# One tile of the way down, from ahead of the third product to behind the fourth, in 18 blocks of a gated MLP

## The chip, the cores and the metric

The kernel runs on one core of one Trainium2 chip. The metric is the device time of one execution in microseconds. The engines of a core run side by side, each through its own list of instructions in order, and wait for one another by semaphores: TensorE (PE in the rows; its weight loads, PEld, overlap with the matmuls), VectorE (DVE), ScalarE (ACT), GpSimd (POOL) and SyncE (SP), which issues the DMAs.

## The reference

One layer of a trunk on x of 1024 tokens by 1024 features in float32: two kinds of attention that share their projections, then a gated MLP. Each part stands behind a norm that is modulated by a conditioning vector. The change lies in the MLP:

```
h = modulate(rms_norm(x), shift_ffn, scale_ffn)
gate, val = split(causal_depthwise_conv(h @ w_up, conv_w, conv_b), 2)   # 2 x 2816 features, width 3 along tokens
x = x + gate_ffn * ((silu(gate) * val) @ w_down)
return rms_norm(x) * final_g
```

## The kernel before

Float32 is kept up by splitting each operand into a high and a low part that TensorE reads as float32r: a product of two operands is three matmuls (high by high, low by high, high by low). `h` lies in SBUF with features on the partitions and tokens along the row, in two halves of 512 tokens, 128 features a piece.

The MLP runs over 22 blocks. Block `fb` makes 128 gate features and 128 value features for all tokens (the way up), applies the convolution, SiLU and the gate, and leaves activations of 128 features by 1024 tokens. These are multiplied with the 128 rows of `w_down` that belong to them (the way down) during the next block. The way down of a block is 16 tiles, each of 128 tokens by 512 output features: three matmuls into a PSUM bank `dnf` (`down_mm`, `mm3g`, L137), and an add of that bank onto `x2` by VectorE (L1231). There are four `dnf` banks, taken in turn.

From block 2 on, the way up of a block (`act_fast`) is a 2 by 2 product (gate and value by two token halves, over two halves of the 1024 input features) done in the manner of Winograd and Strassen: seven products in place of eight. Sums of input halves (`T1`, `T2`, `T4`) are made once, sums of weight quarters for each block by `weight_sums`. A product is 12 matmuls of 128 x 512 (`product`, L1095) into one of four PSUM banks `up`, here called X, Y, W and Z:

- first, into X; ScalarE copies X out (L1121). Second, into Y; VectorE adds it to that copy (L1131), which gives the gate's first token half.
- third, adds into X; ScalarE copies X (L1137). Fourth, adds into X again; ScalarE copies X (L1146).
- fifth, into W; VectorE subtracts it (L1152): the value's first half. Sixth, into Z; VectorE subtracts it (L1162): the value's second half. Seventh, adds into Z; VectorE subtracts it (L1173): the gate's second half.

Behind each of the four results comes its convolution: one pass on ScalarE (L1100) and two on VectorE (L1104). Behind the gate's halves comes SiLU (L1139, L1180). `gated` multiplies gate and value (L1037, VectorE), splits off the high part (L1038, ScalarE) and the low part (L1039, VectorE); for the second token half this is left to the next block, between its first and second product (`rest`).

Between the products stand tiles of the way down of the block before. How many behind which product is a table: entry 0 behind the second product, 1 behind the third, 2 behind the fourth, 3 behind the fifth, 4 behind the sixth; four more stand behind the seventh and none behind the first. Block 2 has its own row of the table (`NTWO`), block 21 too (`NLAST`); the 18 blocks from 3 to 20 use `NDOWN`. The order of the tiles among themselves is fixed: the first four are token tiles 0 to 3 with the first half of the output features, the fifth to eighth the same tokens with the second half, and so on. All of this is kept in the order in which it is written (`ko`).

```
    n = NLAST if last else NTWO if fb == 2 else NDOWN
    ...
    def tiles(n, c=iter(()), dn=dn):
        for _ in range(n):
            nx(dn)
            nx(c)
    ...
    if fb > 2:
        nx(c)
    tiles(n[0], c)
    product(X, w[4], T2, False)
    ko(sc.copy(cg[:, hi], X))
    run(c, 9)
```

`c` is the convolution of the gate's first half: a step of it is taken behind each tile, and what is left of it behind the third product.

Of the kernel before, what the change touches and what calls it, by code (L numbers as in the profile page):

```python
# [26 lines left out]
NP = 8  # L27
FF = 2816
NF = FF // P
NDOWN = 2, 3, 2, 2, 3  # L30
NLAST = 2, 2, 0, 0, 0
NTWO = 0, 4, 2, 3, 3
TL = sum(NLAST)
# [22 lines left out]
def build(nc, tc, t, ctx):  # L56
# [3 lines left out]
    def mk(pool, shape, dt, tag):  # L60
        cnt[0] += 1
        return pool.tile(shape, dt, name=f"{tag}_{cnt[0]}", tag=tag, bufs=BUFS.get(tag, 1))
# [1043 lines left out]
    def act_fast(fb, w, dn, nw, nw1, ld, ld1, act, after, last):  # L1106
# [3 lines left out]
        lo, hi = slice(0, HALF), slice(HALF, S)  # L1110
        n = NLAST if last else NTWO if fb == 2 else NDOWN
        cg, cv = (mk(p2, [P, S], F32, "y") for _ in range(2))
# [379 lines left out]
```

## Time and profile before

| | us |
|---|---|
| median of 3 runs | 1384.16 (1381.42 to 1384.59) |
| the profiled execution | 1383.4 |
| its span, first to last instruction | 1381.6 |
| mean granted TensorE clock | 0.983 of full speed |

The way up and down of the blocks 3 to 20 takes from about 780 us to 1335 us of the span. In rows of the timeline and of the chain the first number is the start in us from the span's start, the second the duration. A matmul's row is longer than its share, as matmuls are pipelined: the distance from one start to the next counts.

### The profile page before, as it was taken

To read this page: it belongs to the slowest core of one execution; us is meant where nothing else is said; L and a number is where in the kernel's file an instruction comes from. 1 tells how busy PE (TensorE), PEld (TensorE's weight loads), DVE (VectorE), ACT (ScalarE), POOL (GpSimd) and SP (SyncE) were. 2 spreads that over 40 slices of the span, in tenths; PEclk is the share of its full clock that TensorE was granted. 3 is DMA by queue.
4 is the path that set the end of the run, shared out by engine and by line. 5 is a ranking of instruction groups with operands and counts; after the bars stand their busy time and mean duration, and the time that the engine had idled before them with its cause. 6 is when DMAs were issued, how large, how long until landed. Compare 5 with 4: busy or idle time off the path is not lost.

```text
span 1381.6 us, 19584 instructions
## 1 busy us (share of the span) xinstructions
PE 1292.6 (94%) x6596; PEld 1072.4 (78%) x6596; DVE 1097.3 (79%) x1896; ACT 651.9 (47%) x1332; POOL 841.2 (61%) x746
## 2 busy tenths in 40 slices
PE   5999999999999979999888999999999999999996
PEld 3897988798788967877666888887888888878874
DVE  7769888788777747857897888888878888888777
ACT  6666656566555544534423333433333334333335
POOL 2157677776543436644686776676667766766754
PEclk9999999999999999999999999999999999999998
DMA  8725444535573586681101111111111111121113
GB/s 332 237 59 137 139 130 124 157 104 145 130 182 105 165 206 209 198 274 61 53 15 46 46 46 59 50 59 63 46 47 46 46 52 56 55 62 53 46 38 123
DMA packets 73169, 145.09 MB, mean 105 GB/s; under 512 B 11114, under 2 KB 21482, under 8 KB 73068
## 3 DMA queue, kind: packets, MB, share of 16 engines
q1 hardware_dynamic: 73068, 143.83, 35.0%
q8 instruction: 53, 0.87, 0.3%
q14 instruction: 48, 0.39, 0.1%
HBM read 103.41 MB, written 18.88 MB: 89 GB/s over the span
## 4 chain that ended last, share of the span: by engine, by line
PE 38%; DVE 29%; ACT 7%; POOL 4%; DMA 4%; issue 3%; SPq 1%; POOLq 0%; ACTq 0%; DVEq 0%
PE up L1095 14%; PE mm L137 9%; PE dnf L137 8%; DVE y L1104 6%; DVE x L1231 4%; PE T L137 4%; DVE y L1037 4%; ACT y L1100 3%; PE S L137 2%; DVE al L1039 2%; ACT ah L1038 1%; POOL pb L780 1%; POOL wl L122 1%; DMA rawm<-ada 1%; DVE y L1282 1%
## 5 line engine op out<-in xcount | busy, mean ns | idle before, releaser
L1231 DVE TENSOR_TENSOR x<-dnf,x 128x512 f32<-128x512 f32 x340 | 226.0, 682 | 10.0 <-PE dnf L137 10.0
L1061 POOL TENSOR_TENSOR wl<-raw,wh 128x1024 fp32r<-128x1024 f32 (+1 forms) x62 | 160.0, 2582 | 76.7 <-ACT wh L1059 75.3
L1095 PE MATMUL up<-h,wh 128*128 128x512 f32 x640 | 202.3, 397 | 1.6 <-ACT y L1137 0.8
L1104 DVE SCALAR_TENSOR_TENSOR y<-y,sm,y 128x512 f32<-128x512 f32 (+2 forms) x160 | 160.9, 1006 | 23.1 <-ACT y L1100 23.1
L137 PE MATMUL mm<-H,wh 128*128 128x512 f32 x448 | 150.2, 403 | 0.0
L137 PE MATMUL dnf<-dh,ah 128*128 128x512 f32 x336 | 134.9, 401 | 14.8 <-DVE x L1231 11.4
L1100 ACT ACTIVATE y<-y,sm 128x512 f32<-128x512 f32 x80 | 65.3, 816 | 176.0 <-DVE y L1152 82.3
L780 POOL TENSOR_TENSOR pb<-pb,kt 128x512 f32<-128x512 f32 (+2 forms) x96 | 102.4, 1080 | 71.2 <-DVE kt L777 48.2
L1095 PEld LDWEIGHTS up<-h,wh 128*128 128x128 f32 x640 | 119.4, 189 | 32.6 <-ACT y L1137 4.6
L137 PE MATMUL dnf<-dh,al 128*128 128x512 f32 x336 | 132.5, 394 | 0.0
L137 PE MATMUL dnf<-dl,ah 128*128 128x512 f32 x336 | 131.5, 391 | 0.0
L1095 PE MATMUL up<-h,wl 128*128 128x512 f32 x320 | 127.2, 397 | 0.0
L800 DVE TENSOR_TENSOR ptl<-T,pth 128x512 fp32r<-128x512 f32 (+2 forms) x192 | 98.5, 515 | 22.4 <-ACT pth L799 20.8
L1209 POOL TENSOR_TENSOR dl<-modt,dh 128x512 fp32r<-128x512 f32 x42 | 56.4, 1342 | 94.1 <-ACT dh L1208 94.1
L773 POOL TENSOR_SCALAR pb<-pb,ri 128x640 f32<-128x640 f32 (+2 forms) x64 | 46.7, 730 | 101.5 <-DVE ri L772 54.4
L799 ACT CAST pth<-T 128x512 fp32r<-128x512 f32 (+2 forms) x192 | 87.4, 457 | 41.2 <-PE T L137 38.9
L137 PE MATMUL T<-ident,pb 128*128 128x128 f32 x528 | 91.3, 277 | 16.0 <-POOL pb L780 5.9
L137 PE MATMUL mm<-wh,H 128*128 128x256 f32 x512 | 99.4, 286 | 3.5 <-DVE vs L481 3.5
L137 PE MATMUL S<-kh,qs 128*128 128x384 f32 (+5 forms) x352 | 98.6, 362 | 3.7 <-ACT pb L756 3.7
L777 DVE TENSOR_TENSOR_SCAN kt<-kt 128x128 f32<-128x128 f32 (+3 forms) x64 | 97.2, 1519 | 6.0 <-ACT kt L762 5.2
L1095 PE MATMUL up<-Tc,wh 128*128 128x512 f32 x320 | 99.5, 392 | 0.0
L1038 ACT CAST ah<-y 128x512 fp32r<-128x512 f32 x42 | 26.1, 621 | 144.1 <-DVE y L1037 144.1
(211 smaller groups left out, 3417.8 us busy)
## 6 DMA issues: line engine op xcount, KB each, us to landing
raw<-w_up SPq DMA_DIRECT2D x44, 512.0 KB, 3.6
rawm<-ada SPq DMA_DIRECT2D x64, 256.0 KB, 3.1
qs<-ex SPq DMA_DIRECT2D x104, 128.0 KB, 2.3
modt<-w_down SPq DMA_DIRECT2D x44, 256.0 KB, 2.6
adaw<-ada SPq DMA_DIRECT2D x16, 512.0 KB, 5.2
raw<-w_qk SPq DMA_DIRECT2D x16, 512.0 KB, 4.4
kh<-ex SPq DMA_DIRECT2D x56, 128.0 KB, 2.6
tbd<-wh SPq DMA_DIRECT2D x18, 256.0 KB, 2.7
```

What stands on the lines that cost most here:

```text
L137: r = fn(*a, **k)
L777: ve.tensor_tensor_scan(r, r, r, 1.0, ALU.mult, ALU.bypass)
L780: gp.tensor_mul(pt[:, a:b], pt[:, a:b], kt[:, a + 1:b + 1])
L799: sc.copy(dh, tp[:, 0:b - a])
L800: ve.tensor_sub(dl, tp[:, 0:b - a], f(dh))
L1037: ko(ve.tensor_mul(yg[:, cc], yg[:, cc], yv[:, cc]))
L1061: late.append(lambda a=a, z=z: ko(gp.tensor_sub(wl[:, a:z], raw[:, a:z], f(wh[:, a:z]))))
L1095: ko(te.matmul(ps, w[x][:, kb], b[kb][y], start=start and n == 0, stop=n == 11, skip_group_check=True))
L1100: ko(sc.activation(y[:, a:z], src[:, a:z], AF.Identity, scale=cw[2][:, b], bias=cb[:, b]))
L1104: ko(ve.scalar_tensor_tensor(y[:, o:z], src[:, o - d:z - d], cw[2 - d][:, b], y[:, o:z], ALU.mult, ALU.add))
L1209: ko(gp.tensor_sub(wl, raw, f(wh)))
L1231: r = ve.tensor_add(xc, ps, xc)
```

## The change

One line of the file: `NDOWN` goes from 2, 3, 2, 2, 3 to 1, 3, 3, 2, 3.

```
--- before.py
+++ after.py
@@ -27,7 +27,7 @@
-NDOWN = 2, 3, 2, 2, 3
+NDOWN = 1, 3, 3, 2, 3
```

A block's tiles remain 16 and keep their order, so which tile stands where shifts by one between the second and the fourth product. TensorE in the first of the middle blocks, behind the second product (`dnf` is a tile's bank, `dh` and `dl` are the high and low parts of the down weights, `ah` and `al` those of the activations, `up` from `Tc` is the third product):

```order
 L137 MATMUL dnf_9214<-dl_9078,ah_9115 128x512
 L137 MATMUL dnf_9214<-dh_9077,al_9117 128x512
-L137 MATMUL dnf_9220<-dh_9077,ah_9115 128x512
-L137 MATMUL dnf_9220<-dl_9078,ah_9115 128x512
-L137 MATMUL dnf_9220<-dh_9077,al_9117 128x512
 L1095 MATMUL up_9164<-Tc_8398,wh_9094 128x512
 L1095 MATMUL up_9164<-Tc_8399,wh_9094 128x512
```

One tile is left ahead of the third product. The same engine a little later, behind the fourth product (`up` from `h`):

```order
 L1095 MATMUL up_9164<-h_1858_7933,wh_9183 128x512
 L1095 MATMUL up_9164<-h_1857_7932,wl_9184 128x512
+L137 MATMUL dnf_9269<-dh_9140,ah_9115 128x512
+L137 MATMUL dnf_9269<-dl_9141,ah_9115 128x512
+L137 MATMUL dnf_9269<-dh_9140,al_9117 128x512
 L137 MATMUL dnf_9274<-dh_9140,ah_9115 128x512
 L137 MATMUL dnf_9274<-dl_9141,ah_9115 128x512
```

Here the block's fifth tile, the first with the second half of the down weights, now opens a group of three; before, it closed the group behind the third product. VectorE in the same block, from the first tile's add on:

```order
 L1231 TENSOR_TENSOR x_1835_7910<-dnf_9214,x_1835_7910 128x512
 L1104 SCALAR_TENSOR_TENSOR y_9194<-y_9168,sm_75,y_9194 128x511
-L1231 TENSOR_TENSOR x_1836_7911<-dnf_9220,x_1836_7911 128x512
 L1104 SCALAR_TENSOR_TENSOR y_9194<-y_9168,sm_75,y_9194 128x510
+L1231 TENSOR_TENSOR x_1836_7911<-dnf_9239,x_1836_7911 128x512
 L1231 TENSOR_TENSOR x_1837_7912<-dnf_9244,x_1837_7912 128x512
 L1231 TENSOR_TENSOR x_1838_7913<-dnf_9249,x_1838_7913 128x512
-L1231 TENSOR_TENSOR x_1835_7910<-dnf_9254,x_1835_7910 128x512
+L1231 TENSOR_TENSOR x_1835_7910<-dnf_9269,x_1835_7910 128x512
```

The second tile's add goes behind the second step of the convolution; the adds keep their order otherwise. On ScalarE and GpSimd the instructions and their order are the same but for the numbers of some weight buffers, and on SyncE they are the same.

## Rows read from the trace of the kernel before

**Rows 1.** The page: busy time, share of the span, instructions of each engine.

```profile
PE 1292.6 (94%) x6596; PEld 1072.4 (78%) x6596; DVE 1097.3 (79%) x1896; ACT 651.9 (47%) x1332; POOL 841.2 (61%) x746
```

**Rows 2.** The chain of waits over one middle block: start us, us, what.

```profile
904.23 2.81 PE up L1095 x12
907.05 1.38 PE dnf L137 x6
908.42 2.73 PE up L1095 x12
...
911.25 0.70 DVE y L1152
...
932.73 0.60 DVE y L1131
...
935.02 1.17 PE up L1095 x5
```

**Rows 3.** Timeline, all engines: start, us, engine line operation, count [idle before <-releaser].

```profile
897.34 1.28 DVE L1231 TENSOR_TENSOR x<-dnf,x 128x512 f32<-128x512 f32 x2
...
902.13 1.29 POOL L1209 TENSOR_TENSOR dl<-modt,dh 128x512 fp32r<-128x512 f32 x1 [0.73 <-ACT dh L1208]
...
902.47 0.68 DVE L1231 TENSOR_TENSOR x<-dnf,x 128x512 f32<-128x512 f32 x1
...
902.64 0.82 ACT L1100 ACTIVATE y<-y,sm 128x512 f32<-128x512 f32 x1 [0.59 <-DVE y L1131]
902.75 0.39 PE L137 MATMUL dnf<-dh,al 128*128 128x512 f32 x1
...
903.29 0.47 PE L137 MATMUL dnf<-dh,ah 128*128 128x512 f32 x1
903.36 0.57 ACT L1137 COPY y<-up 128x512 f32<-128x512 f32 x1
...
903.60 0.39 PE L137 MATMUL dnf<-dl,ah 128*128 128x512 f32 x1
...
903.98 0.30 PEld L1095 LDWEIGHTS up<-h,wh 128*128 128x128 f32 x2 [0.19 <-ACT y L1137]
...
904.55 0.40 PE L1095 MATMUL up<-h,wl 128*128 128x512 f32 x1
```

**Rows 4.** Waits from 740 to 1320 us: us in total, times, longest.

```profile
DVE y L1152 <- PE up L1095: 41.0, 19, 3.2
...
PEld dnf L137 <- issue: 9.5, 18, 0.6
...
PEld up L1095 <- ACT y L1137: 3.4, 18, 0.2
```

**Rows 5.** Timeline of the last block, around its fourth product.

```profile
1334.30 0.56 ACT L1137 COPY y<-up 128x512 f32<-128x512 f32 x1
...
1334.91 0.73 PE L1095 MATMUL up<-h,wh 128*128 128x512 f32 x2 [0.82 <-ACT y L1137]
...
1335.48 0.40 PE L1095 MATMUL up<-h,wl 128*128 128x512 f32 x1
```

**Rows 6.** Timeline of TensorE in block 2, behind its longest wait.

```profile
750.68 0.50 PE L137 MATMUL dnf<-dh,ah 128*128 128x512 f32 x1 [1.87 <-DVE x L1231]
```

**Rows 7.** Stretches: us, busy by engine, granted clock, DMA share, GB/s.

```profile
752.40:755.50 3.10, 3.10 (x9) 2.43 (x8) 1.21 (x3) 1.53 (x2) 0.54 (x1) 0.52 0.20 83
...
1334.90:1337.00 2.10, 2.09 (x9) 1.73 (x10) 2.10 (x5) 0.48 (x1) 0.00 (x0) 1.00 0.45 125
```

**Rows 8.** By tile: ns least/median/most; the page's group: busy us, mean ns.

```profile
L1231 DVE TENSOR_TENSOR x<-dnf,x x340: 673/682/692, 702.3 to 1374.4; 128x512 f32<-128x512 f32 x170
...
L1104 DVE SCALAR_TENSOR_TENSOR y<-y,sm,y x129: 739/755/1508, 811.1 to 1303.7; 128x512 f32<-128x512 f32 x64, 128x511 f32<-128x511 f32 x33, 128x510 f32<-128x510 f32 x32
...
L1104 DVE SCALAR_TENSOR_TENSOR y<-y,sm,y 128x512 f32<-128x512 f32 (+2 forms) x160 | 160.9, 1006 | 23.1 <-ACT y L1100 23.1
```

## The prediction, on record before the run

> **What bounds the kernel now.** I read the page first [rows 1]: TensorE is busy for 94% of the span and VectorE for 79%. That says which engines matter, and not which of them sets the time, so I went to the chain of waits in order of time over one middle block [rows 2]. The reader is to see a closed lap there. The fourth product starts at 904.23, two tiles of the way down follow (1.38 us), then the fifth product. As soon as this one ends, VectorE starts L1152 at 911.25. From there the chain runs on VectorE with short trips to ScalarE (gated product L1037, sum L1131) and comes back to TensorE only at the next block's fourth product, at 935.02. The lap is 935.02 - 904.23 = 30.79 us, and the chain shows it again in every middle block.
>
> Next I read all engines in order of time around the return to TensorE [rows 3]. Matmuls start about 0.23 us apart (six of the tiles in 1.38 us, twelve of a product in 2.73 to 2.81 [rows 2]). The third tile behind the third product is the exception: it starts 0.54 us after the matmul ahead of it (902.75 to 903.29), and its second matmul 0.31 later (903.60). That loses 0.31 + 0.08 = 0.39 us. Three things end close together at this place. One is VectorE's add of the block's first tile (902.47 + 0.68 = 903.15): there are four banks for these tiles, so the fifth tile of a block, which is this one, waits for the first one's bank. The second is GpSimd's low part of the second half of the down weights (902.13 + 1.29 = 903.42), which the fifth tile is the first to use. The third is ScalarE's copy L1137 (903.36 + 0.57 = 903.93): it reads the bank into which the fourth product goes on adding, and the fourth product's weight load starts at 903.98, marked as having waited for it. The list of waits over the whole stretch [rows 4] has both marks 18 times: 9.5 us ahead of that tile's weight load, and 3.4 us for L1137. So all 18 middle blocks look alike, and TensorE by itself would do a block in 30.79 - 0.39 = 30.40 us.
>
> **The change part by part.** It touches the blocks 3 to 20, 18 of them. In each, one tile (three matmuls on TensorE and one add on VectorE) goes from ahead of the third product to behind the fourth. It issues no DMA; SyncE's order is the same, and on ScalarE and GpSimd only buffer numbers differ. No instruction is added.
>
> Ahead of the third product: it starts 0.69 us sooner. It needs nothing late. What it adds into was filled by the first product, long copied out. The three tiles behind it are now the block's second to fourth. Their banks are free at the latest with the adds that began at 897.34 and took 1.28 us [rows 3], some 2 us before. So the 0.39 us stall goes: the fifth tile now stands behind the fourth product, when its bank and the weights have been there for 3 us.
>
> What is late next: L1137, which was only 0.5 us behind the stall's end. It starts when L1100 ahead of it on ScalarE is done (902.64 + 0.82), and that one waited for L1131 on VectorE, by its row. Nothing in the order of L1131, L1100 and L1137 changes, and the chain runs from L1152 up to them without TensorE [rows 2]. So the fourth product starts at the same point of the lap as now. TensorE comes to it earlier and waits. The last block shows this already, as it has only two tiles between these products: copy done at 1334.30 + 0.56 = 1334.86, and 0.82 us idle before the fourth product [rows 5]. Restarting after the longer wait costs nothing more: from the end of the copy to the third matmul it is 1335.48 - 1334.86 = 0.62 there and 904.55 - 903.93 = 0.62 in a middle block [rows 3, 5].
>
> Behind the fourth product: three tiles stand between it and the fifth, for which L1152 waits. Queued behind L1152 on VectorE is all the rest of the lap. Two tiles take 1.38 us [rows 2], a third one 0.69. The whole of it lies on the lap: the fifth product ends 0.69 later after the fourth began, L1152 starts 0.69 later, and so does everything up to the next copy. The sixth product, for which L1162 waits, shifts as much, so no second path stays short. New lap: 30.79 + 0.69 = 31.48 us, with TensorE waiting 31.48 - 30.40 = 1.08 us in each for the copy.
>
> Cover elsewhere: the moved add takes no longer (adds take 673 to 692 ns whatever else runs [rows 8]), and VectorE has time for it: it already stands idle ahead of L1152 until the fifth product ends, 41.0 us in 19 blocks [rows 4], some 2.2 us each. The second of the two convolution steps (L1104) behind the second product comes one add earlier, so SiLU and GpSimd's first weight work of the block come up to 0.9 us earlier as well. Between that and L1152 VectorE does only adds from PSUM. From L1152 on GpSimd's work is set off by casts that follow L1152 and L1162 on ScalarE, so it moves along with them.
>
> The price of that GpSimd overlap is not seen directly. L1104 takes 739 to 1508 ns, with a mean of 1006 over 160 of them, which is eight in each of 20 blocks [rows 8]; so 8 x (1006 - 739) = 2.1 us of a block hang on what runs beside it. From below: a better overlap could give the 0.69 back and more, down to TensorE's own 30.40. From above: a worse one could cost as much again. I take zero, because the order of GpSimd against VectorE is unchanged wherever both use SBUF.
>
> The Trainium skill's "SBUF — State Buffer", section "SBUF: two separate sides", says that a VectorE operation with two SBUF inputs and a GpSimd operation exclude each other for a whole instruction. The trace agrees in that the adds from PSUM do not vary while L1104 doubles. By that rule also the lap changes only if the change makes them meet otherwise.
>
> **Sum.** 18 laps by 0.69 us = 12.4 us (a tile of 0.68, three of the shortest matmul steps of 2.73 / 12, would give 12.3). Ahead of block 3 nothing differs, and the last block, whose fourth product waits for its copy already, passes the delay on in full. The profiled execution took 1383.4 us (span 1381.6), 0.8 under the median of the runs shown and inside their spread of 3.2. 1383.4 + 12.4 = 1395.8.
>
> **Rivals.**
> A, faster. The bank of the fifth tile is what holds TensorE; with it free, TensorE paces the lap. Each lap loses its 0.39: 18 x 0.39 = 7.0 us, 1376.4. For it: the stall repeats 18 times and its mark is the larger of the two [rows 4]. The Trainium skill's "Perfetto Trace Analysis", section "Optimization Strategy", reads a gap that repeats as too little room for the next tile, which is this reading; the trace agrees that a bank is waited for. It decides only if the fourth product could begin before 903.93 in lap time, and [rows 3, 5] show it held by the copy both with and without the stall. Chance 4%.
> B, no change. The 0.69 is taken back on VectorE's leg because GpSimd's earlier start makes the overlaps shorter; 0.69 of the 2.1 us would be enough for 1383.4, and with up to 0.23 of it left in each of the 18 laps the time is 1383 to 1387.5. Against it: the part of GpSimd that moves meets only adds. 6%.
> C, much slower. The new 1.08 us waits bring TensorE's clock down. In block 2, behind a wait of 1.87 us and six matmuls [rows 6], the granted clock was 0.52 for 3.1 us [rows 7], about the lower of its two levels (1.2 and 2.4 GHz), which lost 3.1 x 0.48 = 1.5 us. Once in each lap, behind the wait for the copy and so on the lap, that would be 18 x (0.69 + 1.5) = 39.4 us, 1422.8. Against it: about the last block's wait of nearly the same size the clock stayed at 1.00 [rows 7]. 3%.
>
> **How the numbers follow.** Forecast 87%, A 4%, B 6%, C 3%. The likeliest is 1395.8. Its own range is 1392 to 1399: runs of one kernel spread by 3.2 us, and a lap that is off by 0.1 us makes 1.8 in all. To 1390 below it takes in a partial B, to 1400 above a slightly worse overlap. About what these runs can tell from no change is 0.3%, 4.2 us. Faster: A, 4%. Same: B, 6%. Slower: the rest, 90%.
>
> **What would show it.** Right: middle blocks 31.5 us apart from fourth product to fourth product; the wait of some 0.5 us ahead of a tile gone; a wait of about 0.8 to 1.3 us for L1137 ahead of each fourth product; VectorE idle 0.7 us more per block, ahead of the adds behind the fourth product; the durations of L1104 and L1037 as now; granted clock 1.00. Wrong: a lap under 30.8 us, or a fourth product that starts before L1137 has ended (A); a lap as now with shorter L1104 or L1037 (B); a granted clock below 1.00 behind the wait (C).

## The result: 0.7% slower, and the profile after

| | before | changed |
|---|---|---|
| median, us | 1384.38 | 1394.12 (1391.81 to 1399.46) |
| ratio to before | | 1.0072, 95% interval 1.0048 to 1.0096 |
| profiled execution, us | 1383.4 | 1394.73 |
| its span, us | 1381.6 | 1393.0 |

One of the six executions of before took 1799.16 us; it counts in the median of the table, and the ratio leaves it out (median 1384.16 of the other five).

The chain of waits of the changed kernel, over one middle block (start us, us, what):

```profile
904.99 0.47 ACT y L1137
905.47 0.04 issue
905.51 3.07 PE up L1095 x12
908.58 2.06 PE dnf L137 x9
910.64 2.73 PE up L1095 x12
...
913.47 0.70 DVE y L1152
...
934.94 0.61 DVE y L1131
...
935.64 0.82 ACT y L1100
936.46 0.47 ACT y L1137
...
936.98 0.73 PE up L1095 x2
```

The lap is 936.98 - 905.51 = 31.47 us, against 30.79 in [rows 2]. Between the fourth and the fifth product there are nine matmuls of the way down and 2.06 us, where there were six and 1.38. From L1152 to L1131 it is 21.47 us, as in [rows 2] (21.48). What else changed is the way back to TensorE: the chain now goes from L1131 through L1100 and the copy L1137, and no tile stands on it.

The timeline of the same place, all engines:

```profile
904.17 0.82 ACT L1100 ACTIVATE y<-y,sm 128x512 f32<-128x512 f32 x1 [0.59 <-DVE y L1131]
904.26 0.39 PE L137 MATMUL dnf<-dh,al 128*128 128x512 f32 x1
904.90 0.56 ACT L1137 COPY y<-up 128x512 f32<-128x512 f32 x1
...
905.02 1.54 DVE L1104 SCALAR_TENSOR_TENSOR y<-y,sm,y 128x511 f32<-128x511 f32 x2 [0.35 <-ACT y L1100]
905.51 0.30 PEld L1095 LDWEIGHTS up<-h,wh 128*128 128x128 f32 x2 [1.28 <-ACT y L1137]
905.51 0.73 PE L1095 MATMUL up<-h,wh 128*128 128x512 f32 x2 [0.86 <-ACT y L1137]
...
906.08 0.40 PE L1095 MATMUL up<-h,wl 128*128 128x512 f32 x1
```

TensorE is done with the three tiles at 904.26 and stands until the copy has ended at 904.90 + 0.56 = 905.46. From there to the third matmul it is 906.08 - 905.46 = 0.62 us, as in [rows 3, 5]. The waits from 740 to 1330 us (us in total, times, longest):

```profile
DVE y L1152 <- PE up L1095: 37.8, 18, 2.1
...
PEld up L1095 <- ACT y L1137: 22.5, 18, 1.3
...
DVE x L1231 <- PE dnf L137: 17.2, 18, 1.0
PE up L1095 <- ACT y L1137: 14.9, 18, 0.9
```

Against [rows 4], the 18 stalls of 9.5 us ahead of a tile are gone, and the weight load's 3.4 us for L1137 are 22.5. That is 1.25 us each; as the matmul sees it, 0.83.

The stretch with the 18 laps (us, busy by engine, granted clock, DMA share, GB/s), and durations by tile in ns, least, median, most:

```profile
811.11:1345.98 534.87, 520.35 (x2244) 420.03 (x2244) 440.11 (x545) 200.35 (x289) 354.74 (x204) 1.00 0.16 50
```

```profile
L1231 DVE TENSOR_TENSOR x<-dnf,x x340: 672/681/694, 701.8 to 1385.8; 128x512 f32<-128x512 f32 x170
```

```profile
L1104 DVE SCALAR_TENSOR_TENSOR y<-y,sm,y x126: 749/968/1500, 810.6 to 1298.6; 128x512 f32<-128x512 f32 x62, 128x511 f32<-128x511 f32 x32, 128x510 f32<-128x510 f32 x32
```

The clock stayed at 1.00 throughout, and adds and convolution steps take what they took [rows 8]. For L1104 the median is to be read with care, as its durations lie in two groups and the middle one jumps between them: 755 ns of 129 in that row, 967 of 128 in the kernel before from 811 to 1300 us, 968 of 126 here. The means of its three shapes there are 1155, 751 and 965 ns before and 1162, 751 and 972 here.

Where the 11.4 us between the two spans are: the fourth product of block 3 and that of the last block start here in the changed kernel,

```profile
779.64 0.50 PE L1095 MATMUL up<-h,wh 128*128 128x512 f32 x1 [0.39 <-ACT y L1137]
...
1345.98 0.50 PE L1095 MATMUL up<-h,wh 128*128 128x512 f32 x1 [0.83 <-ACT y L1137]
```

and in the one before at 780.90 and at 1334.91 [rows 5]. The 18 laps are 566.34 us against 554.01, 12.33 more. Ahead of the first of these starts the changed kernel's execution was 1.26 us shorter, and behind the last fourth product some 0.3 longer. The first of these is chance: up to L1131 of block 3 the two programs are the same, but from the tile that waits in block 2 [rows 6] to there it took 28.02 us in the execution of before, where the clock went down [rows 7], and 26.12 in this one, where it did not (last section); the waiting tile itself had come 0.73 us later here.

### The profile page after: what moved, and what is told of

Read it like the earlier page. It is cut to its first block, busy times and chain, and to the rows that moved or that the text cites. A ratio compares the mean times of both kernels' runs of the same rounds, so it can differ in the third digit from the quotient of the medians.

```text
span 1393.0 us, 19566 instructions
## 1 busy us (share of the span) xinstructions
PE 1289.6 (93%) x6596; PEld 1071.8 (77%) x6596; DVE 1101.0 (79%) x1896; ACT 653.6 (47%) x1332; POOL 841.2 (60%) x746
## 4 chain that ended last, share of the span: by engine, by line
DVE 37%; PE 27%; ACT 10%; POOL 4%; DMA 3%; issue 3%; SPq 1%; POOLq 0%; ACTq 0%; DVEq 0%
DVE y L1104 9%; PE mm L137 9%; PE up L1095 8%; DVE x L1231 6%; DVE y L1037 6%; ACT y L1100 5%; PE T L137 4%; PE dnf L137 3%; DVE al L1039 2%; PE S L137 2%; ACT ah L1038 2%; POOL wl L122 1%; DMA rawm<-ada 1%; DVE y L1162 1%; DVE y L1152 1%
## 5 line engine op out<-in xcount | busy, mean ns | idle before, releaser
L1061 POOL TENSOR_TENSOR wl<-raw,wh 128x1024 fp32r<-128x1024 f32 (+1 forms) x62 | 160.0, 2581 | 69.6 <-ACT wh L1059 64.5
L1104 DVE SCALAR_TENSOR_TENSOR y<-y,sm,y 128x512 f32<-128x512 f32 (+2 forms) x160 | 161.7, 1011 | 23.8 <-ACT y L1100 23.1
L1100 ACT ACTIVATE y<-y,sm 128x512 f32<-128x512 f32 x80 | 65.3, 816 | 186.1 <-DVE y L1152 93.4
L1038 ACT CAST ah<-y 128x512 fp32r<-128x512 f32 x42 | 26.1, 621 | 142.5 <-DVE y L1037 142.5
```

The costliest lines, as they stand in the source:

```text
L1061: late.append(lambda a=a, z=z: ko(gp.tensor_sub(wl[:, a:z], raw[:, a:z], f(wh[:, a:z]))))
L1100: ko(sc.activation(y[:, a:z], src[:, a:z], AF.Identity, scale=cw[2][:, b], bias=cb[:, b]))
L1104: ko(ve.scalar_tensor_tensor(y[:, o:z], src[:, o - d:z - d], cw[2 - d][:, b], y[:, o:z], ALU.mult, ALU.add))
```

## The experiments

The theory: the middle blocks are one closed lap, from the fourth product over the tiles behind it and the fifth product to L1152, along VectorE to L1131, and over L1100 and L1137 back to the fourth product. A tile behind the fourth product lengthens it. Laps below are from the fourth product of one middle block to that of the next, in each kernel's profile; "before" is timed anew beside each group of runs.

**Each half of the change alone.** First, the tile leaves the place ahead of the third product but goes behind the third:

```
-NDOWN = 2, 3, 2, 2, 3
+NDOWN = 1, 4, 2, 2, 3
```

> Table 1, 4, 2, 2, 3: the tile leaves the place ahead of the third product, as in the change, but goes behind the third product; behind the fourth there are two as before. Theory (the lap runs from the fourth product over the tiles behind it, the fifth product, VectorE's leg and copy L1137 to the next fourth product): lap 30.79 us as before, total within 2 us of before, and the stall ahead of the fifth tile, now the fourth behind the third product, still there. Rival (the delay comes from what is taken from ahead of the third product, or from the two convolution steps that stand side by side on VectorE): lap 31.47, 12.3 us slower.

Measured: 1385.99 us, ratio 1.0014 (0.9990 to 1.0039). Timeline of TensorE at the fifth tile, and the fourth products of two blocks:

```profile
904.93 0.47 PE L137 MATMUL dnf<-dh,ah 128*128 128x512 f32 x1 [0.16 <-DVE x L1231]
...
905.69 0.43 PE L1095 MATMUL up<-h,wh 128*128 128x512 f32 x1
...
936.46 0.43 PE L1095 MATMUL up<-h,wh 128*128 128x512 f32 x1
```

The lap is 30.77 and the stall is there. What is taken from ahead of the third product costs nothing and gives nothing.

Second, the tile goes from behind the third to behind the fourth:

```
-NDOWN = 2, 3, 2, 2, 3
+NDOWN = 2, 2, 3, 2, 3
```

> Table 2, 2, 3, 2, 3: two tiles stay ahead of the third product, one goes from behind the third to behind the fourth. Theory: lap 31.47 us as in the changed kernel, 12.3 us slower than before, 22 us in all of waiting for L1137. Rival (the place ahead of the third product): lap 30.79 or, with the bank stall gone, 30.40, that is 0 to 7 us faster.

Measured: 1400.79 us, ratio 1.0117 (1.0074 to 1.0160). Two fourth products:

```profile
905.37 0.73 PE L1095 MATMUL up<-h,wh 128*128 128x512 f32 x2 [0.83 <-ACT y L1137]
...
936.83 0.50 PE L1095 MATMUL up<-h,wh 128*128 128x512 f32 x1 [0.82 <-ACT y L1137]
```

The lap is 31.46, the changed kernel's: 18 x 0.67 = 12.1 us, so in the laps this half is the whole of it. The ratio stands for 16 us; it comes from four executions between 1394.6 and 1405.7, and what the rest of it is was not looked for.

**Twice the cost.**

```
-NDOWN = 2, 3, 2, 2, 3
+NDOWN = 1, 2, 4, 2, 3
```

> Table 1, 2, 4, 2, 3: a second tile goes behind the fourth product, taken from behind the third. Theory: each tile there adds its whole time to the lap, 31.47 + 0.69 = 32.15 us, 12.3 us over the changed kernel's laps; TensorE waits 1.8 us a lap for L1137 and its clock stays at 1.00 if waits of this length do not bring it down. Rival (the changed kernel's delay comes from the place ahead of the third product): lap 31.47. Rival (longer waits bring the clock down): lap over 33 us and a granted clock under 1.00.

Measured: one run, 1404.77 us beside 1386.32 of before. Two fourth products, and the lap between them as a stretch (columns as above):

```profile
906.00 0.50 PE L1095 MATMUL up<-h,wh 128*128 128x512 f32 x1 [1.52 <-ACT y L1137]
...
938.14 0.50 PE L1095 MATMUL up<-h,wh 128*128 128x512 f32 x1 [1.52 <-ACT y L1137]
```

```profile
906.00:938.13 32.13, 30.61 (x132) 24.71 (x132) 25.98 (x33) 11.79 (x17) 20.84 (x12) 1.00 0.15 50
```

The lap is 32.14 us, 0.67 over the changed kernel, as forecast to 0.01. TensorE stood 1.5 us for the copy in each lap at a clock of 1.00.

**The hold taken away.** If the copy holds the fourth product because it stands behind L1100 on ScalarE, then putting it ahead should free TensorE. The convolution of the gate's first half is no longer begun ahead of the third product:

```
 c = conv_steps(yg, cg, fb, 0, HALF)
-if fb > 2:
-    nx(c)
-tiles(n[0], c)
+tiles(n[0])
 product(X, w[4], T2, False)
 ko(sc.copy(cg[:, hi], X))
 run(c, 9)
```

With the changed kernel's table:

> The changed kernel, with ScalarE's first convolution pass (L1100) of the gate's first half moved behind copy L1137 in every block from 3 on, and both VectorE steps behind the tiles ahead of the third product. Theory: L1137 no longer follows VectorE's sum L1131, the bank stall is gone already, so TensorE paces the blocks by itself: lap 30.40, no wait for L1137; 7.0 us under before by the 18 laps and up to 1 us more from the last block, so about 1376; 19 to 20 us under the changed kernel. Rival (the delay of the changed kernel is not the copy's): lap stays at 31.47 and the total at 1394 to 1396.

Measured: ratio 0.9935 (0.9908 to 0.9963) to before, 1378.32 us. Copy and fourth product, and the fourth product of the block ahead:

```profile
906.09 0.39 PE L1095 MATMUL up<-h,wh 128*128 128x512 f32 x1
...
935.40 0.58 ACT L1137 COPY y<-up 128x512 f32<-128x512 f32 x1
...
936.42 0.39 PE L1095 MATMUL up<-h,wh 128*128 128x512 f32 x1
```

The lap is 30.33, 0.07 under what I had worked out for TensorE alone, and the copy ends 0.44 us before it is needed. The wait for L1137 is not in the list any more. So the tile behind the fourth product is not slow in itself: it was slow on a closed lap. The edit takes VectorE's two steps of that convolution along; that they are not the gain by themselves is seen from the same edit with the other table, which follows.

With the table of before:

> The kernel before (table 2, 3, 2, 2, 3) with the same move of L1100 behind L1137. Theory: before has two holds at one place, the copy and the fifth tile's bank, both set by VectorE's L1131; with the copy free the bank still holds, lap 30.75 to 30.79, total 0 to 2 us under before. Rival (the copy alone held the kernel before): lap 30.40, 7 to 8 us faster.

Measured: 1383.86 us, ratio 0.9997 (0.9976 to 1.0018). Copy, fifth tile and fourth product:

```profile
904.32 0.58 ACT L1137 COPY y<-up 128x512 f32<-128x512 f32 x1
...
904.83 1.27 DVE L1231 TENSOR_TENSOR x<-dnf,x 128x512 f32<-128x512 f32 x2
...
905.65 0.47 PE L137 MATMUL dnf<-dh,ah 128*128 128x512 f32 x1
...
906.42 0.63 PE L1095 MATMUL up<-h,wh 128*128 128x512 f32 x2
...
937.21 0.40 PE L1095 MATMUL up<-h,wh 128*128 128x512 f32 x1
```

The copy is over at 904.90, but the fifth tile waits for the bank that the first of the two adds frees (904.83 + 0.68 = 905.51), and the lap stays at 30.79. Before had two holds, and taking away one of them does not free TensorE: in the changed kernel the bank's is gone and the copy holds, in this one the copy's is gone and the bank holds. Both together gave 0.46 us a lap.

How long the freed copy's slack lasts:

```
 (copy first, as above)
-NDOWN = 1, 3, 3, 2, 3
+NDOWN = 1, 2, 4, 2, 3
```

> Table 1, 2, 4, 2, 3 with the copy L1137 ahead of L1100, as in the kernel with the copy first. There the copy was done 0.44 us before the fourth product began, at a lap of 30.33. Theory: the fourth tile behind the fourth product moves VectorE's leg, and with it the copy, 0.69 later against TensorE; 0.44 of it is covered, the rest and some 0.1 of the semaphore show: lap 30.6 to 30.7. Rival (with the copy ahead of L1100 the place of the tile no longer matters at all): lap 30.33.

Measured: one run, 1385.73 us beside 1386.32; two fourth products:

```profile
906.20 0.74 PE L1095 MATMUL up<-h,wh 128*128 128x512 f32 x2 [0.15 <-ACT y L1137]
...
936.97 0.50 PE L1095 MATMUL up<-h,wh 128*128 128x512 f32 x1 [0.15 <-ACT y L1137]
```

30.77 us. The copy holds again, so the rival falls; the lap is 0.07 over the upper end of my estimate, and I did not look for what makes that up.

**One tile fewer behind the fourth product.**

```
-NDOWN = 2, 3, 2, 2, 3
+NDOWN = 2, 3, 1, 2, 4
```

> Table 2, 3, 1, 2, 4: one tile is taken away from behind the fourth product and put behind the sixth. Theory: the lap loses the tile's 0.69 on TensorE and gains its add of 0.60 on VectorE, because behind the sixth product VectorE's leg is on the lap: 30.79 - 0.69 + 0.60 = 30.70 us, the total within 2 us of before. Rival (only TensorE's part between fourth and fifth product counts): TensorE's own pace of 30.40 or less, 7 us faster.

Measured: one run, 1377.33 us beside 1386.32; two fourth products:

```profile
904.12 0.39 PE L1095 MATMUL up<-h,wh 128*128 128x512 f32 x1
...
934.48 0.39 PE L1095 MATMUL up<-h,wh 128*128 128x512 f32 x1
```

The lap is 30.36, TensorE's pace, and not 30.70. My theory was wrong in one leg: the add that went onto VectorE's leg did not cost its 0.60. The place is the gated product L1037 of the first half. In the kernel before:

```profile
919.47 2.85 POOL L1061 TENSOR_TENSOR wl<-raw,wh 128x1024 fp32r<-128x1024 f32 x1
...
920.58 2.29 DVE L1037 TENSOR_TENSOR y<-y,y 128x512 f32<-128x512 f32 x1
```

and with the add ahead of it:

```profile
918.83 2.86 POOL L1061 TENSOR_TENSOR wl<-raw,wh 128x1024 fp32r<-128x1024 f32 x1
920.54 1.70 DVE L1037 TENSOR_TENSOR y<-y,y 128x512 f32<-128x512 f32 x1
```

In both L1037 ends 0.55 us behind GpSimd's operation (922.87 and 922.32; 922.24 and 921.69). It starts 0.60 later against GpSimd and takes 0.59 less. A test in a kernel where TensorE waits, so that the lap shows VectorE's leg alone:

```
-NDOWN = 1, 3, 3, 2, 3
+NDOWN = 1, 2, 3, 2, 4
```

> Table 1, 2, 3, 2, 4: as the changed kernel, but one tile goes from behind the third product to behind the sixth. TensorE waits for the copy in this kernel, so the lap shows VectorE's leg alone. With one tile taken from behind the fourth product, the add behind the sixth had not cost its 0.60: the gated product L1037 started 0.60 later against L1162, took 1.70 us in place of 2.29, and ended 0.55 us behind GpSimd's low part of the weights, as before. New theory: L1037 is held until that GpSimd operation ends, so an add ahead of it is free and the lap is 31.47 again. Rival (every add on the leg counts, and the other kernel had gained elsewhere): 31.47 + 0.60 = 32.07.

Measured: one run, 1391.88 us beside 1386.23 of before. Two fourth products, and L1037 with GpSimd's operation:

```profile
902.74 0.50 PE L1095 MATMUL up<-h,wh 128*128 128x512 f32 x1 [0.86 <-ACT y L1137]
...
918.91 2.86 POOL L1061 TENSOR_TENSOR wl<-raw,wh 128x1024 fp32r<-128x1024 f32 x1
920.62 1.70 DVE L1037 TENSOR_TENSOR y<-y,y 128x512 f32<-128x512 f32 x1
...
934.20 0.50 PE L1095 MATMUL up<-h,wh 128*128 128x512 f32 x1 [0.86 <-ACT y L1137]
```

31.46 us: the add is free, and L1037 again ends 0.55 behind GpSimd (922.32 and 921.77).

**The faster versions, timed.** The table with one tile behind the fourth product:

> Table 2, 3, 1, 2, 4 again, now timed against the kernel before. Its lap was 30.36, TensorE's own pace. Theory: 18 x (30.79 - 30.36) = 7.7 us and 0.7 in the last block, 8 us under before: ratio 0.994. Rival (the run with the profile was a lucky one): ratio within 0.2% of 1.

Measured: 1377.22 us, ratio 0.9935 (0.9918 to 0.9952).

The same table and the copy first:

> Table 2, 3, 1, 2, 4 and the copy L1137 ahead of L1100. Theory: TensorE already paces the middle blocks in either, so the two do not add: lap 30.33 to 30.36, at most 1 us from the last block; ratio 0.993 to 0.994. Rival (each gives its own 7 us): lap under 30.1, ratio 0.989.

Measured: 1376.23 us, ratio 0.9929 (0.9913 to 0.9945); the lap is 30.36. The two ways do not add. Both this and the plain table beat the kernel before and the changed one; between them the runs do not decide.

## Why the prediction was right, step by step

The forecast was 1395.8 us and a slower kernel; the median is 1394.12, inside the likeliest case's range. That the totals lie so close is in part luck: the range was built on runs that spread by 3.2 us, and those of the changed kernel spread by 7.7. The medians moved by 10.0 us (from 1384.16), the laps by 12.33, and it is the laps that bear the forecast out.

- **The lap as the bound.** Right. Doubling the tile adds the same again (32.14), and each half alone gives what its place on the lap says (30.77 and 31.46).
- **18 x 0.69 us.** 12.4 forecast, 12.33 measured in the 18 laps. The whole execution moved by less, 11.3 to 1394.73, because the part ahead of them came out 1.26 us shorter, by the clock in block 2.
- **The stall goes and the copy is late next.** Right: no stall, and 18 waits of 1.25 us (0.83 at the matmul) where 0.8 to 1.3 was said. The kernels with the copy first show it from both sides: with the bank's stall gone the copy alone held TensorE, with the copy free the bank alone did. TensorE's own pace was put a little too high, 30.40 against 30.33.
- **Restart at no cost.** Right, 0.62 us again.
- **GpSimd's overlap taken as zero.** Right for this change: L1104's mean over the kernel is 1011 ns against 1006, and L1037's median from 811 to 1300 us is 1995 against 1994. The bound was put too narrowly, though. I priced L1104 with its 2.1 us and put no price on L1037, which the lap contains twice and which gave 0.59 in another table. Rival B, a gain on VectorE's leg by another meeting with GpSimd, did not happen here, but its mechanism is real.
- **VectorE idle 0.7 us more per block ahead of the adds.** Half right. The wait of the adds for their tiles is 17.2 us in 18 blocks, 0.96 each, and had been 0.48; so 0.5, not 0.7. The other 0.2 is not idling: VectorE is busy for 25.89 us in the lap above (905.51 to 936.98) and for 25.71 in that of before (904.07 to 934.86), with 33 operations in either.
- **Rival A** fell with the wait for L1137 at each fourth product, **rival C** with the clock at 1.00, also at the 1.5 us waits of the doubled version.

## What to carry to other kernels

When a chain of waits closes on itself once per block, an instruction's cost depends on whether it lies on that lap: the same tile was worth 0.69 us behind one product, nothing two places earlier, and nothing behind the same product with the copy moved ahead, until a further tile used up the slack. Before moving work to remove a visible stall, list everything that ends within a microsecond of it; here three possible holds ended within 0.8 us, and removing the bank's left the copy's. The cheapest gain was the opposite move: a tile off the lap, to a place where its VectorE part stands ahead of an operation that waits anyway.

## What the runs showed of the hardware

**VectorE held by GpSimd.** L1037 ended 0.55 us behind the same GpSimd operation in three kernels, whether it had started 1.11, 1.71 or 1.71 us into it, and took 2.29 or 1.70 us. Its least duration in the changed kernel is 673 ns. The Trainium skill's "SBUF — State Buffer", section "SBUF: two separate sides", says that the one which comes second waits for the whole operation of the other; these ends agree. The second half's L1037 ends as far behind the block's other L1061, at 931.03 against 930.48 in the kernel before. No run moved GpSimd's operation by itself. In the two tables with one more add ahead of L1037, the add of 0.60 us was free: L1037 would have stood for that time anyway.

**The clock, by chance.** In block 2 TensorE stands for 1.8 to 1.9 us between the fourth product and the tiles behind it, in the kernel before [rows 6] as in the eleven others. The table with one tile behind the fourth product was profiled twice; the same stretch from 740 to 800 us, first and second profile (us, busy by engine, granted clock, DMA):

```profile
740.00:800.00 60.00, 57.13 (x246) 45.62 (x245) 46.79 (x62) 23.16 (x33) 42.27 (x26) 1.00 0.16 49
```

```profile
740.00:800.00 60.00, 57.18 (x238) 45.23 (x238) 47.70 (x62) 20.75 (x30) 39.55 (x23) 0.97 0.18 55
```

The clock of the same program fell towards the lower of its two levels (1.2 and 2.4 GHz) in one execution, to 0.52 from 751 to 754 us, and not in the other. In the kernel before it fell too [rows 7], in the changed one it did not. The twelve profiles can be laid side by side, as their programs are the same up to L1131 of block 3: from the waiting tile to there it took 28.0 to 28.2 us in the eight where the clock fell, and 26.1 to 26.6 in the four where it stayed. Waits of 0.9 to 1.5 us in every lap never did that. A microsecond or two between two profiles can be this alone, which is why the laps were compared and not the spans.
